# The first scale and shift as TensorE products in four column tiles, and two projection units multiplied tile by tile

## Chip, cores and metric

One NeuronCore of a Trainium2 chip runs the whole program. The metric is device time in microseconds (us) of one execution.

## The reference

A trunk of two layers, 256 tokens of 1024 channels, all in float32. What the change touches is the beginning of layer 0:

```python
cond = jax.nn.silu(c)
for l in range(DEPTH):
    sh1, sc1, g1, sh2, sc2, g2 = jnp.split(cond @ ada_w[l] + ada_b[l], 6, axis=-1)
    hn = rmsnorm(x, norm_mix_w[l]) * (1.0 + sc1[:, None]) + sh1[:, None]
...
        mix = mixer_ab(hn, ab_w_in[e], ...)
    x = x + g1[:, None] * mix
```

`mixer_ab` projects `hn` with `ab_w_in`, runs attention with sinks on one part and a gated DeltaNet on another (a short causal convolution with SiLU on q, k and v, then the delta rule in chunks of 64), and projects back. A dense SwiGLU, a second mixer, a top-2-of-8 expert SwiGLU and a final norm follow.

## The kernel before

All weights stream from HBM in units of 1 MB (128 partitions of 2048 floats) through five `raw` buffers. One queue, SyncE's (SP), issues every load in program order, and a load waits until the unit that was in its buffer has been read. The engines each run their instructions in order; a scheduler sets that order from the program and its own estimates, except inside `manual_schedule`, where the program's order stands.

A float32 product is made of three products of 32-bit halves. `split` makes the halves of a weight: ACT casts `raw` to `hi` (128x1024 at a time), DVE subtracts to get `lo` (two pieces of 128x512). `mm3` then issues hi by hi, lo by hi and hi by lo. The norm's output is kept as eight channel tiles (128 channels by 256 tokens), each again as `xhi` and `xlo`. So a unit of 256 output channels costs two halves of 8 tiles by 3 products, 48 matmuls.

At the start, `ada_first` makes the first scale (`Ac`) and shift (`shc`), two channel tiles at a time. The weight unit lies in HBM transposed (`adaw`), and DVE multiplies it by the SiLU row `crow` and sums along the row, one instruction per channel tile with `junk` as its output. `norm_T` is interleaved with this by its `before` callback: it scales x by the root mean square into `xs0` and `xs1`, PE turns each channel tile (two transposes into a PSUM tile `cb`), ACT writes `xhi` from it with scale and shift, ACT (for tiles 0 to 3) or DVE (4 to 7) writes the float32 `fk`, and DVE subtracts for `xlo`.

`mixer_ab` then multiplies unit by unit: first the small unit `abs` (beta and decay inputs, 24 products, since it fills one half), then the two k units (`abw[1]`, `abw[2]`), whose `sink` copies the result to `cpad`, applies the four convolution taps (one on ACT, three on DVE, `cv`), SiLU and the squares for the l2 norm. From the small unit come beta and g by a softplus of some twenty small DVE instructions, and from g the decay matrices `DT`; k and `DT` go into the `pair` products, and a long chain of small steps that inverts a triangular matrix follows. The q, v and attention units are fillers, pumped into that chain.

## Time and profile before

| | |
|---|---|
| median of 3 runs | 1418.18 us (1418.10 to 1418.77) |
| the profiled execution | 1417.63 us |
| its span in the trace | 1415.80 us |
| PE, DVE, ACT busy | 1349.7, 971.5, 727.6 us |
| mean rate from HBM | 340 GB/s |

The span runs from the first to the last instruction of the trace; 1.83 us of the execution lie around it. Times in the trace count from the start of the span. A matmul's time in a row holds its way through the array, so that the spacing of two matmuls' starts, not their length, is what one costs in a stream.

### The profile page before, as it was taken

What the parts mean: (1) busy time and instruction counts of PE and PEld (TensorE: products, weight loads), DVE (VectorE), ACT (ScalarE), POOL (GpSimd) and SP (SyncE); (2) the same over time, 40 slices, a digit from 0 to 9 for tenths busy, and PEclk for the clock granted to TensorE, in tenths of its full rate; (3) what the DMA queues carried; (4) which work ended last, traced back from release to release, by engine and by line L of the source; (5) the groups of instructions that cost most, each with busy time, mean ns of one, the idle gap of its engine ahead of it and who ended that gap; (6) DMA issues with size and microseconds to landing.
All of it is one profiled execution on the core that took longest, in us unless ns stands there. A gap on an engine that the chain in (4) does not pass through costs nothing.

```text
span 1415.8 us, 22845 instructions
## 1 busy us (share of the span) xinstructions
PE 1349.7 (95%) x8894; PEld 1031.7 (73%) x8894; DVE 971.5 (69%) x1373; ACT 727.6 (51%) x1003; POOL 13.0 (1%) x25
## 2 busy tenths in 40 slices
PE   2989998999989999999999999999999999999996
PEld 1888677999979986687666766667766677666762
DVE  7899878878987965787556665557655567465542
ACT  5865527444457754676444554445544555344531
POOL 0010000000000000000000000000000000000000
PEclk9999999999999999999999999999999999999998
DMA  9548356879773423999999999999999999999994
GB/s 374 200 153 323 124 187 265 319 284 409 298 273 135 148 91 119 383 426 426 425 426 424 425 426 425 426 425 427 424 426 426 425 426 425 427 425 426 424 426 191
DMA packets 68662, 482.71 MB, mean 341 GB/s; under 512 B 7873, under 2 KB 8257, under 8 KB 10689
## 3 DMA queue, kind: packets, MB, share of 16 engines
q1 hardware_dynamic: 66816, 477.19, 82.4%
q10 hardware_dynamic: 1728, 3.97, 0.8%
q8 instruction: 72, 1.18, 0.3%
q14 instruction: 46, 0.37, 0.1%
HBM read 479.03 MB, written 2.10 MB: 340 GB/s over the span
## 4 chain that ended last, share of the span: by engine, by line
PE 86%; DVE 8%; ACT 3%; issue 1%; DMA 1%; SPq 0%; ACTq 0%; DVEq 0%
PE gu L1426 14%; PE gu L219 10%; PE gu L221 10%; PE gu L220 10%; PE dnh L1448 7%; PE dn L219 5%; PE dn L221 5%; PE dn L220 5%; PE pj L221 3%; PE pj L219 2%; PE pj L220 2%; PE ms L1476 2%; DVE lo L205 1%; DVE ajunk L248 1%; PE cb L221 1%
## 5 line engine op out<-in xcount | busy, mean ns | idle before, releaser
L205 DVE TENSOR_TENSOR lo<-raw,hi 128x1024 fp32r<-128x1024 f32 (+1 forms) x496 | 578.5, 1178 | 188.1 <-ACT hi L200 178.8
L200 ACT CAST hi<-raw 128x1024 fp32r<-128x1024 f32 x473 | 490.7, 1049 | 339.6 <-DMA raw<-in_md 101.6
L1426 PE MATMUL gu<-raw,xq 128*64 128x256 f32 x1792 | 207.5, 382 | 0.0
L219 PE MATMUL gu<-hi,xeh 128*128 128x512 f32 x448 | 181.0, 404 | 0.0
L1426 PEld LDWEIGHTS gu<-raw,xq 128*64 128x64 f32 x1792 | 125.1, 137 | 75.1 <-issue 18.5
L220 PE MATMUL gu<-lo,xeh 128*128 128x512 f32 x448 | 177.6, 396 | 0.0
L221 PE MATMUL gu<-hi,xel 128*128 128x512 f32 x448 | 177.4, 396 | 0.0
L221 PE MATMUL pj<-xhi,lo 128*128 128x256 f32 x376 | 107.2, 287 | 6.5 <-DVE lo L205 6.3
L219 PE MATMUL pj<-xhi,hi 128*128 128x256 f32 x376 | 107.2, 286 | 5.4 <-ACT hi L200 5.4
L220 PE MATMUL pj<-xlo,hi 128*128 128x256 f32 x376 | 106.8, 285 | 0.0
L1448 PE MATMUL dnh<-raw,hq 128*64 128x512 f32 x448 | 103.6, 600 | 0.5 <-ACT hq L1480 0.5
L219 PEld LDWEIGHTS gu<-hi,xeh 128*128 128x128 f32 x448 | 84.4, 188 | 21.2 <-issue 3.0
L219 PE MATMUL gu<-xhi,hi 128*128 128x256 f32 x352 | 99.5, 283 | 0.0
L221 PE MATMUL gu<-xhi,lo 128*128 128x256 f32 x352 | 99.0, 281 | 0.4 <-DVE lo L205 0.4
L221 PEld LDWEIGHTS gu<-hi,xel 128*128 128x128 f32 x448 | 84.5, 189 | 20.3
L232 DVE SCALAR_TENSOR_TENSOR ajunk<-raw,crow 128x1024 bf16<-128x1024 f32 x80 | 98.5, 1231 | 0.9
L220 PE MATMUL gu<-xlo,hi 128*128 128x256 f32 x352 | 98.9, 281 | 0.0
L220 PEld LDWEIGHTS gu<-lo,xeh 128*128 128x128 f32 x448 | 84.6, 189 | 18.2
L1469 DVE TENSOR_TENSOR h<-sg,gu 128x256 f32<-128x256 f32 (+1 forms) x56 | 30.8, 550 | 87.2 <-PE gu L221 78.8
L219 PE MATMUL dn<-hi,hh 128*128 128x512 f32 x224 | 90.1, 402 | 0.0
L220 PE MATMUL dn<-lo,hh 128*128 128x512 f32 x224 | 87.5, 391 | 0.0
L221 PE MATMUL dn<-hi,hl 128*128 128x512 f32 x224 | 87.5, 391 | 0.0
(450 smaller groups left out, 1872.8 us busy)
## 6 DMA issues: line engine op xcount, KB each, us to landing
raw<-in_mg SPq DMA_DIRECT2D x112, 1024.0 KB, 19.5
raw<-in_mu SPq DMA_DIRECT2D x112, 1024.0 KB, 19.5
raw<-in_md SPq DMA_DIRECT2D x110, 1024.0 KB, 19.5
raw<-in_adaw SPq DMA_DIRECT2D x48, 1024.0 KB, 8.9
raw<-in_fgu SPq DMA_DIRECT2D x22, 1024.0 KB, 7.5
raw<-in_cdw SPq DMA_DIRECT2D x14, 1024.0 KB, 5.5
raw<-in_fdn SPq DMA_DIRECT2D x11, 1024.0 KB, 7.1
raw<-in_abw SPq DMA_DIRECT2D x9, 1024.0 KB, 7.8
```

The source lines that it names most:

```text
L200: self.nc.scalar.copy(hv, src)
L205: self.nc.vector.tensor_tensor(lv[z], src[z], hv[z].bitcast(F32), op=ALU.subtract)
L219: mm(ps, lh, rh, start=first, stop=False)
L220: mm(ps, lh, rl, start=False, stop=False)
L221: mm(ps, ll, rh, start=False, stop=last)
L232: nc.vector.scalar_tensor_tensor(junk, raw[:, h], 1.0, self.crow, op0=ALU.mult, op1=ALU.mult, accum_out=dst[:, q:q + 1])
L248: nc.vector.scalar_tensor_tensor(junk, raw[:, h], 1.0, self.crow, op0=ALU.mult, op1=ALU.mult, accum_out=dst[:, 2 * u + h:2 * u + h + 1])
L1426: nc.tensor.matmul(gu[name, i][q * HALF:q * HALF + HALF, 0:256], xf[:, kk], w[:, k, q * 256:q * 256 + 256], start=kk == 0, stop=kk == 7)
L1448: nc.tensor.matmul(acc[e][h * HALF:h * HALF + HALF], st[i][:, k % 2, k // 2 * HALF:k // 2 * HALF + HALF], w[:, 0, h * 512:h * 512 + 512], ...
L1469: nc.vector.tensor_tensor(h, st[i], gu.pop(('mu', i))[:, 0:m], op=ALU.mult)
L1476: nc.tensor.transpose(ps[:, q], h[:, q * P:(q + 1) * P], ident)
```

## The change

The scale and shift weights of the first norm now lie in HBM as they do for a projection (`adaf`, channels by 256 outputs). `ada_first` multiplies them on PE: for each of the eight channel blocks one float32 matmul whose stationary operand is the block's SiLU column, broadcast to 32 columns, so that block k goes to column tile k mod 4 and to a quarter of the PSUM partitions. ACT copies the 256 sums out (`asum`), and a matmul of one column with `sums` (ones on partitions 0, 32, 64 and 96) adds the four quarters and turns them into a column. DVE adds the bias.

`first` replaces the interleaved `norm_T`. Under `manual_schedule` it goes through four rounds: scale and shift of two channel tiles, their transposes, `xhi` and `xlo`, then those tiles' products with the two k units, which are loaded ahead of the small unit. Their sums stay open in four PSUM tiles (three `pj` and the one `ms`) over all rounds. `mixer_ab` gets the finished sums as `begun`, and the small unit comes after them. All eight `fk` and both halves of `xs1` are DVE's now.

```diff
+    A['adaf'] = blocks(f['ada_w'][0][:, :2 * D], 256)
...
-    def ada_first(self, A, sh):
+    def ada_first(self, wk, u, A, sh, sums):
...
-        for u in range(4):
-            z = slice(2 * u, 2 * u + 2)
-            for j, dst in ((1, A), (0, sh)):
-                raw = self.raw(self.A['adaw'][j * 4 + u])
-                for h in range(2):
-                    junk = self.ap.tile([P, D], BF16, name="ajunk", bufs=1)
-                    nc.vector.scalar_tensor_tensor(junk, raw[:, h], 1.0, self.crow, op0=ALU.mult, op1=ALU.mult,
-                                                   accum_out=dst[:, 2 * u + h:2 * u + h + 1])
...
+        for i, (j, dst) in enumerate(((1, A), (0, sh))):
+            raw = self.first_raw.pop(0)
+            h = slice(i * 256, i * 256 + 256)
+            for k in range(8):
+                q = slice(k % 4 * 32, k % 4 * 32 + 32)
+                nc.tensor.matmul(ps[q, h], self.cc[:, k:k + 1].to_broadcast([P, 32]), raw[:, k], start=k < 4, stop=k >= 4)
+            nc.scalar.copy(sb[:, h], ps[:, h])
+            for c in range(2 * i, 2 * i + 2):
+                nc.tensor.matmul(pc[:, c:c + 1], sb[:, c * P:(c + 1) * P], sums, start=True, stop=True)
+            nc.vector.tensor_tensor(dst[:, z], pc[:, 2 * i:2 * i + 2], self.col('ada', j * 8 + 2 * u, 2), op=ALU.add)
...
+    def first(self, wk, A, sh):
...
+        todo = [W['adaf'][4], W['adaf'][0], W['abw'][1], W['adaf'][5], W['adaf'][1], W['abw'][2],
+                W['adaf'][6], W['adaf'][2], W['adaf'][7], W['adaf'][3]]
...
+        def tile_(k):
+            p = turned.pop(k)
+            fk = wk.tile([P, T], F32, name="fk", tag="Ub", bufs=2)
+            nc.scalar.activation(hi[:, k], p, AF.Identity, bias=sh[:, k:k + 1], scale=A[:, k:k + 1])
+            nc.vector.tensor_scalar(fk, p, A[:, k:k + 1], sh[:, k:k + 1], op0=ALU.mult, op1=ALU.add)
+            nc.vector.tensor_tensor(lo[:, k], fk, hi[:, k].bitcast(F32), op=ALU.subtract)
+
+        def halves(u):
+            for s in range(2):
+                w.append(self.split(units[u][:, :, s * P:s * P + P]))
+
+        def times(k, us):
+            for u in us:
+                for i in (2 * u, 2 * u + 1):
+                    hv, lv = w[i]
+                    self.mm3(ps[i], (hv[:, k], lv[:, k]), (hi[:, k], lo[:, k]), k == 0, k == 7)
+
+        with self.tc.manual_schedule():
+            self.ada_first(wk, 0, A, sh, sums)
+            fetch(2)
+            turn(0), turn(1)
+            tile_(0), tile_(1)
+            halves(0)
+            fetch(1)
+            times(0, (0,)), times(1, (0,))
+            self.ada_first(wk, 1, A, sh, sums)
+            fetch(2)
+            turn(2), turn(3)
+            tile_(2), tile_(3)
+            times(2, (0,)), times(3, (0,))
+            halves(1)
+            for k in range(4):
+                times(k, (1,))
+            self.ada_first(wk, 2, A, sh, sums)
+            turn(4), turn(5)
+            tile_(4), tile_(5)
+            times(4, (0, 1)), times(5, (0, 1))
+            turn(6), turn(7)
+            self.ada_first(wk, 3, A, sh, sums)
+            tile_(6), tile_(7)
+            times(6, (0,)), times(7, (0,)), times(6, (1,)), times(7, (1,))
...
-        kn, gk = conv_in(0, 1, "kn", rk)
+        kn, sink = conv_in(0, 1, "kn", rk)
+        for u in range(2):
+            sink(u, begun[u])
         small()
-        for _ in gk:
-            pass
...
-                xT = self.norm_T(wk, Ac, shc, busy=True, before=before)
-                self.mixer_ab(xT, wk, g1, Ac2, shc2)
+                xT, begun = self.first(wk, Ac, shc)
+                self.mixer_ab(xT, begun, wk, g1, Ac2, shc2)
```

The order of the instructions shows three places. Numbers behind a name are buffers. First PE, in the kernel before: after the last transposes of the norm come the products of the small unit (`hi_262`, `lo_263`), one channel tile after the other.

```order
L309 MATMUL cb_240<-konst_71,xs1_146 128x128
L309 MATMUL cb_247<-konst_71,xs0_145 128x128
L309 MATMUL cb_247<-konst_71,xs1_146 128x128
L219 MATMUL pj_267<-xhi_151,hi_262 128x256
L220 MATMUL pj_267<-xlo_152,hi_262 128x256
L221 MATMUL pj_267<-xhi_151,lo_263 128x256
```

PE in the changed kernel, second round: the scale's eight products (`raw_123`), the two with `sums`, the shift's (`raw_125`), four transposes, and then the products of tiles 2 and 3 with the first k unit (`hi_202`, `hi_207`).

```order
L249 MATMUL cb_226<-raw_123,cc_81 32x256 x8
L252 MATMUL cb_228<-sums_127,asum_227 128x1 x2
L249 MATMUL cb_226<-raw_125,cc_81 32x256 x8
L252 MATMUL cb_228<-sums_127,asum_227 128x1 x2
L292 MATMUL cb_261<-konst_71,xs0_142 128x128
L292 MATMUL cb_261<-konst_71,xs1_143 128x128
L292 MATMUL cb_264<-konst_71,xs0_142 128x128
L292 MATMUL cb_264<-konst_71,xs1_143 128x128
L217 MATMUL pj_150<-xhi_148,hi_202 128x256
L218 MATMUL pj_150<-xlo_149,hi_202 128x256
L219 MATMUL pj_150<-xhi_148,lo_203 128x256
```

What was one block of transposes and one block of products is cut into rounds; each `L252` reads the `asum` that ACT copies from the `cb` of the row ahead of it.

Second, DVE where the norm ends. Before, the small unit's halves (`lo_263`) lie between the last weight sums, and the first k unit's (`lo_305`, `lo_334`) directly behind the last two norm tiles, with the small unit's result (`ab`).

```order
L248 SCALAR_TENSOR_TENSOR ajunk_223,shc_89<-raw_219,crow_75 128x1024
L205 TENSOR_TENSOR lo_263<-raw_260,hi_262 128x512
L250 TENSOR_TENSOR shc_89<-shc_89,colp_72 128x2
L205 TENSOR_TENSOR lo_263<-raw_260,hi_262 128x512
L315 TENSOR_SCALAR fk_243<-cb_240,Ac_88,shc_89 128x256
L315 TENSOR_SCALAR fk_250<-cb_247,Ac_88,shc_89 128x256
L316 TENSOR_TENSOR xlo_152<-fk_243,xhi_151 128x256
L316 TENSOR_TENSOR xlo_152<-fk_250,xhi_151 128x256
L205 TENSOR_TENSOR lo_305<-raw_299,hi_304 128x512
L425 COPY ab_255<-cb_294 128x32
```

In the changed kernel the same place has the last two norm tiles, the small unit's halves (`lo_504`), both k units' convolutions, and only then the halves of the next unit (`lo_699`, `lo_728`) and the small unit's result.

```order
L253 TENSOR_TENSOR shc_89<-cb_395,colp_72 128x2
L298 TENSOR_SCALAR fk_421<-cb_387,Ac_88,shc_89 128x256
L299 TENSOR_TENSOR xlo_149<-fk_421,xhi_148 128x256
L298 TENSOR_SCALAR fk_425<-cb_390,Ac_88,shc_89 128x256
L299 TENSOR_TENSOR xlo_149<-fk_425,xhi_148 128x256
L203 TENSOR_TENSOR lo_504<-raw_501,hi_503 128x512 x2
L471 SCALAR_TENSOR_TENSOR cv_459<-cpad_460,colp_72,cv_459 128x256 x6
L471 SCALAR_TENSOR_TENSOR cv_459<-cpad_480,colp_72,cv_459 128x256 x6
L203 TENSOR_TENSOR lo_699<-raw_696,hi_698 128x512 x2
L203 TENSOR_TENSOR lo_728<-raw_696,hi_727 128x512 x2
L506 COPY ab_455<-cb_535 128x32
```

The convolutions moved ahead of the small unit's result and of the next unit's halves. Third, ACT in the changed kernel's last two rounds and behind them.

```order
L250 COPY asum_322<-cb_321 128x256 x2
L297 ACTIVATE xhi_148<-cb_349,shc_89,Ac_88 128x256
L297 ACTIVATE xhi_148<-cb_352,shc_89,Ac_88 128x256
L640 ACT_TABLE_LOAD
L640 ACTIVATE ea_569<-rowp_74 128x8
L250 COPY asum_394<-cb_393 128x256 x2
L297 ACTIVATE xhi_148<-cb_387,shc_89,Ac_88 128x256
L297 ACTIVATE xhi_148<-cb_390,shc_89,Ac_88 128x256
L198 CAST hi_503<-raw_501 128x1024
L465 COPY cpad_460<-pj_150 128x256
L469 ACTIVATE cv_459<-pj_150,colp_72 128x256
```

The cast of the small unit (`raw_501`) stands behind the last tile of the norm, and the copies of the k units' results behind it.

## Rows read from the trace of the kernel before

**Rows 1.** The page: busy tenths in 40 equal slices, 35.4 us each.
```profile
PE   2989998999989999999999999999999999999996
```

**Rows 2.** Chain of waits in order of time: start us, us, what.
```profile
1.67 6.29 DMA x<-in_x
...
10.73 1.15 DVE ajunk L248 x2
...
33.06 1.22 DVE ajunk L248 x2
...
34.94 0.58 PE pj L221
...
38.09 0.21 PE pj L219
...
38.82 0.12 PE pj L220
...
564.03 9.46 DMA raw<-in_mg
...
652.52 3.60 PE gu L1426 x32
```

**Rows 3.** Stretch, length, busy us (instructions) of PE, PEld, DVE, ACT, POOL; granted clock, DMA.
```profile
55.00:60.00 5.00, 5.00 (x49) 4.91 (x48) 4.52 (x12) 4.30 (x6) 2.12 (x3) 1.00 0.25 100
60.00:65.00 5.00, 5.00 (x45) 5.00 (x44) 3.58 (x10) 4.96 (x9) 0.87 (x1) 1.00 0.51 162
65.00:70.00 5.00, 5.00 (x19) 2.61 (x18) 3.86 (x8) 4.94 (x6) 0.10 (x1) 1.00 0.11 48
70.00:100.00 30.00, 26.07 (x299) 23.38 (x299) 30.00 (x65) 18.72 (x29) 3.80 (x4) 1.00 0.38 128
...
sum 95.00, PE 90.76 PEld 83.60 DVE 87.75 ACT 65.11 POOL 10.18; mean PE 10.08 PEld 9.29 DVE 9.75 ACT 7.24 POOL 1.13
```

**Rows 4.** Timeline: start us, us, engine line op out<-in xcount [idle before <-releaser].
```profile
11.85 0.29 ACT L286 ACTIVATE rstd<-rstd,eps 128x2 f32<-128x2 f32 x1
13.25 0.72 ACT L297 ACTIVATE xs<-x,rstd 128x512 f32<-128x512 f32 x1 [1.11 <-DVE rstd L287]
16.23 0.56 ACT L311 ACTIVATE xhi<-cb,shc,Ac 128x256 fp32r<-128x256 f32 x1 [0.42 <-PE cb L309]
17.29 0.43 DVE L316 TENSOR_TENSOR xlo<-fk,xhi 128x256 fp32r<-128x256 f32 x1
29.05 0.54 DVE L315 TENSOR_SCALAR fk<-cb,Ac,shc 128x256 f32<-128x256 f32 x1
29.11 1.04 ACT L200 CAST hi<-raw 128x1024 fp32r<-128x1024 f32 x1
34.88 0.68 DVE L205 TENSOR_TENSOR lo<-raw,hi 128x512 fp32r<-128x512 f32 x1
39.44 0.36 ACT L421 COPY abT<-pj 16x256 f32<-16x256 f32 x1 [2.43 <-PE pj L221]
39.85 0.29 PE L424 MATMUL cb<-konst,abT 16*128 16x16 f32 x2 [0.22 <-ACT abT L421]
51.59 0.57 ACT L381 COPY cpad<-pj 128x512 f32<-128x512 f32 x1
54.10 2.46 DVE L390 SCALAR_TENSOR_TENSOR cv<-cpad,colp,cv 128x256 f32<-128x256 f32 x6
432.21 1.10 PE L987 MATMUL cb<-xc,lga 128*128 128x256 f32 x4
```

**Rows 5.** Busy time by stretch while the first weights land (columns as in rows 3).
```profile
10.00:15.00 5.00, 0.97 (x4) 0.65 (x5) 4.32 (x11) 3.87 (x7) 0.00 (x0) 1.00 1.01 424
```

**Rows 6.** Busy time by stretch around a change of the granted clock (PEclk).
```profile
154.80:158.20 3.40, 1.54 (x12) 1.24 (x12) 2.72 (x8) 3.34 (x10) 0.00 (x0) 0.97 0.40 169
158.20:161.60 3.40, 3.40 (x16) 1.82 (x16) 2.14 (x6) 2.23 (x6) 0.00 (x0) 0.53 0.02 5
161.60:165.00 3.40, 3.40 (x46) 2.39 (x45) 1.89 (x4) 0.66 (x2) 0.00 (x0) 1.00 0.36 84
```

More of the change, by code (lines that the diff above doesn't have):

```diff
@@ new lines, in first, with fetch, turn @@
+    def first(self, wk, A, sh):
+        nc, W = self.nc, self.A
+        nc.sync.dma_start(self.x, W['x'])
+        todo = [W['adaf'][4], W['adaf'][0], W['abw'][1], W['adaf'][5], W['adaf'][1], W['abw'][2],
+                W['adaf'][6], W['adaf'][2], W['adaf'][7], W['adaf'][3]]
+        self.first_raw, units = [], []
+        def fetch(n):
+            for _ in range(n):
+                src = todo.pop(0)
+                (units if len(todo) in (7, 4) else self.first_raw).append(self.raw(src))
+            if not todo:
+                self.late()
+        fetch(5)
+        sums = wk.tile([P, 1], F32, name="sums")
+        nc.vector.tensor_reduce(sums, self.kc('ident')[:, 0:P:32], axis=AX.X, op=ALU.add)
+        r = self.rstd(wk)
+        xs = [wk.tile([P, D], F32, name=f"xs{t}", tag=tg) for t, tg in enumerate(("kbe", "kdec"))]
+        for h in range(2):
+            hs = slice(h * 512, h * 512 + 512)
+            nc.scalar.activation(xs[0][:, hs], self.x[:, 0, hs], AF.Copy, scale=r[:, 0:1])
+            nc.vector.tensor_scalar(xs[1][:, hs], self.x[:, 1, hs], r[:, 1:2], None, op0=ALU.mult)
+        hi = self.xtp.tile([P, 8, T], F32R, name="xhi", tag="xhi")
+        lo = self.xtp.tile([P, 8, T], F32R, name="xlo", tag="xlo")
+        ps = [self.psp.tile([P, 512], F32, name="pj", bufs=3)[:, 0:T] for _ in range(3)]
+        ps.append(self.psm.tile([P, 512], F32, name="ms")[:, 0:T])
+        w = []
+        turned = {}
+        def turn(k):
+            turned[k] = self.psp.tile([P, T], F32, name="cb", bufs=4)
+            for t in range(2):
+                nc.tensor.transpose(turned[k][:, t * P:(t + 1) * P], xs[t][:, k * P:(k + 1) * P], self.kc('ident'))
+        def tile_(k):
[36 more added lines that the diff above has]
+            times(6, (0,)), times(7, (0,)), times(6, (1,)), times(7, (1,))
+        return (hi, lo), (ps[:2], ps[2:])
@@ L288, in rstd, with norm_T @@
         return r
-    def norm_T(self, pool, Acol, shcol, tags=("kbe", "kdec"), busy=False, before=None):
+    def norm_T(self, pool, Acol, shcol, tags=("kbe", "kdec")):
         nc = self.nc
@@ L380, in sink @@
                 nc.gpsimd.memset(pad[:, :, 0:3], 0.0)
-                nc.scalar.copy(pad[:, :, 3:], ps)
+                if b:
+                    nc.scalar.copy(pad[:, :, 3:], ps)
                 us = slice(2 * u, 2 * u + 2)
@@ L384, in sink @@
                     q = 2 * u + s
+                    p = ps[:, s] if b else ps[s]
+                    if not b:
+                        nc.scalar.copy(pad[:, s, 3:], p)
                     def w(tap):
                         return self.col('dnc', tap * 12 + w0 * 4 + q)
-                    nc.scalar.activation(cv[:, q], ps[:, s], AF.Copy, scale=w(3))
+                    nc.scalar.activation(cv[:, q], p, AF.Copy, scale=w(3))
                     for tap in range(3):
@@ L406, in sink @@
                         nc.vector.reciprocal(nrm, nrm)
-            return cv, self.proj_chan([A['abw'][1 + 2 * b + v] for v in range(2)], xT, sink)
+            return cv, sink if b == 0 else self.proj_chan([A['abw'][1 + 2 * b + v] for v in range(2)], xT, sink)
         va = wk.tile([P, 2, P], F32, name="va")
```

31 lines of the change are left out of this document (9 added, 22 removed).

## Prediction

> **What bounds the kernel now.** I read the page's slices first [rows 1]: PE is at 9 or more tenths nearly everywhere, and the first slice of 35 us holds the one long stretch in which it has almost nothing to do. The whole change lies there. The chain of waits over that stretch [rows 2] says what is waited for: x lands at 7.96, its squares run on ACT, and from 10.73 to 34.28 it is DVE alone, with sixteen products of adaLN weights by the silu row (`ajunk`, two to a scale or shift of two channel tiles). PE's steady stream of projection products begins at 34.94. From there, two things are to be seen. Products of 256 columns follow each other every 0.21 us at first, which is 1.2 GHz, and every 0.12 us from about 38.5, which is 2.4 GHz [rows 2]; the column of the granted clock reads 1.00 in all of that stretch, and I go by the spacing. And the engines are all full: the windows from 35 to 130 us [rows 3] show DVE at 30.00 of 30.00 us from 70 to 100 and at 87.75 of the 95 in all. So after 35 the stage is paid in DVE time, with PE close behind, and a gain at the start counts only as far as DVE and PE reach the same state sooner. Such a shift reaches the end in full: the first expert weights are waited for at 564 [rows 2], after a routing that needs everything ahead of it.
>
> The state to compare is the one in which all eight norm tiles, the small unit (`abs`, 24 products) and the two k units (96 products) are done. Before, ACT starts to copy the second k unit out at 51.59 [rows 4], so these 120 products end at about 51.5.
>
> **What is removed.** DVE's sixteen products of 1.22 us, some 20 us, and with them the queue in which a norm tile's low part waited behind them. DVE gets xs1 (two halves, about 0.45 us each) and all eight `fk` instead of four. Both lie where DVE now waits.
>
> **What is added on PE.** For each weight unit (eight of them) there are eight f32 matmuls of 256 columns in four column tiles, one ACT copy, two matmuls of one column, and small DVE adds. No row shows four tiles. The nearest are one tile, four matmuls of this shape in 1.10 us, about 0.235 us apart [rows 4], and two tiles, 32 in 3.60 us, 0.1125 us each at 2.4 GHz [rows 2]. Doubling the tiles halved the price, so I take 0.056 us at 2.4 GHz and 0.11 us at 1.2 GHz; the other end is that four tiles run no better than two. Eight then take 0.45 or 0.86 us. Behind them come some 0.25 us until the result is out and seen, 0.37 us for the copy (0.36 for `abT`, and 0.05 from its end to PE's next start), and 0.3 us for the two short ones (0.29 for the pair of L424) [rows 4]. One half is 1.35 us at 2.4 GHz and 1.85 us at 1.2 GHz. The rows of the order show why nothing fills it: PE runs in order, and L252 stands directly behind its own eight, waiting for ACT.
>
> The Trainium skill, "TensorE: Matmul & The Clock Gate", section "Measured speedup vs the span model", measures 2.38 times for three column tiles, not 3. By it four tiles would make about 3.2 times, an estimate, and the 64 matmuls would cost 1 to 2 us more; the sum below would be about +5 instead of +3.7. No row here shows four tiles.
>
> **The start, step by step.** The weights are not late. A unit is 1.05 MB, the queue moves 424 GB/s [rows 5], so units land about 2.5 us apart after x's 7.96: 10.4, 12.9, and so on to about 32.8 for the last scale-or-shift unit. The first of them waits for ACT: the root is done at 12.14, then come the reciprocal and two xs halves (0.72 us each, about 0.62 apart) [rows 4], and in ACT's order the first copy stands behind these, at 13.6. From there, by rows 4 (xhi 0.56, fk 0.54, xlo 0.43, cast 1.04, lo 0.68 us):
> Round 1: second half done at 16.2; four transposes; first low tile at 18.4; the first unit's casts stand behind two xhi on ACT (17.8 to 19.8), its low parts on DVE come at 19.8 and 21.0; twelve products until 22.5.
> Round 2: two halves at 1.85 us to 26.2; transposes; low tile at 28.4; twelve products to 30.8; then 24 products of the other unit. These 36 are the first stretch in which PE is full, so I let the clock rise at about 32; they end at 34.2.
> Round 3: two halves at 1.35 us to 36.9; low tile 38.8; 24 products, partly at 1.2 GHz, to 43.1.
> Round 4: transposes, two halves to 46.2; low tiles to 48.9; 24 products to 51.0.
> Then the small unit's 24 (2.8 us) to 53.8. So the 120 products end about 2.3 us later than now, although the first began 15 us earlier: half of the time between 13.6 and 51 PE waits for a copy, an add or a tile.
>
> The clock is the weak term. The windows around 158 [rows 6] show what PE did before it fell and rose here: with 1.54 of 3.40 us busy it fell from 2.4 to 1.2 GHz, and after a stretch that was full it was back. Rounds 3 and 4 are of the first sort in part. With 1.2 GHz for all four rounds, the same steps end at 58.3; with 2.4 GHz for all of them at 45.8.
>
> **The sum.** DVE's ledger, since DVE is the full engine. Work between 35 and 130 before: 87.75 us [rows 3]. Of it, done in the changed kernel by the last low tile: eight lo halves of the k units (5.0 us) and two fk and two xlo (1.7 us). Of the small unit's two lo, about 0.75 us ran before 35 and is now still to do. Left: 81.8 us. From 48.9 that reaches 130.7, against 130: +0.7 us if DVE never waits again. It will: between 55 and 70 it is idle for 15.00 - 4.52 - 3.58 - 3.86 = 3.04 us, in the chain from the small unit through g and the decay matrices [rows 3]. That chain starts at 39.4 now (`abT`) [rows 4], and at 53.8 after the change, behind the k units rather than ahead of them, with less other work to lay beside it. I let 3.0 us recur: **+3.7 us**. All 7.25 us of idle between 35 and 130 would make +8.0. A second account agrees in sign: in DVE's new order twelve convolution steps (2.46 us for six [rows 4]) stand ahead of the next unit's lo, so PE, done with the small unit at 53.8, waits until about 57 for work that it has at 51.6 now; against that, six of those steps are done sooner.
>
> The profiled execution took 1417.63 us and the median of the runs is 0.55 us above it. 1417.63 + 3.7 is 1421.3, so the median should be **1421.9 us**, 0.26% slower. Below about 0.2% (2.8 us) a measurement of this kernel can't be told from no change.
>
> **The rivals.**
> *Clock at 1.2 GHz throughout, or tiles that don't overlap.* The first makes the rounds end at 58.3, the second (0.1125 us a matmul) at 53 to 58: +6 to +11 us, up to 1429. For it: the clock fell at 158 after a stretch with waits in it, and the rounds are made of such stretches [rows 6]. Against it: the 36 products of round 2 are as full as the stretch at 35 after which the clock rose. Chance 0.15. The Trainium skill, the same page, section "HAM oscillation — how this bites in real kernels", speaks against the change: bursts of matmuls between waits each begin at the low clock. The rise and fall around 158 agree.
> *Clock at 2.4 GHz from the second round on, DVE's waits as before.* Rounds end at 45.8 to 47, the last low tile at 43.7 to 45: the ledger gives -1.5 to 0 us, about 1417.5, no change that can be measured. Chance 0.20.
> *The same clock, and DVE's waits vanish*, since the k units' convolutions and the next splits now fill the gaps of the chain from the small unit. 43.7 + 81.8 is 125.5: -4.5 us, 1413.7, faster by 0.3%. It decides as soon as the last low tile comes before about 45 and DVE is never idle for more than a microsecond until 130. For it: 33 more projection products stand ahead of the first pair products of the delta rule in the new order. Against it: those three idle microseconds are waits for ACT and POOL, which no DVE order fills. Chance 0.15.
> That the change does nothing can be left out: the order shows every instruction moved.
>
> **How the numbers follow.** My forecast (rounds ending between 49 and 53, +1 to +7 us, 1419 to 1425) has 0.45, the three rivals 0.15, 0.20 and 0.15; 0.05 is for none of these. Slower by over 0.2%: most of the forecast (0.38), the first rival, a little of the rest, 0.54. Within 0.2%: the second rival and the low end of the forecast, 0.29. Faster: the third rival and the rest, 0.17. The range from 1415 to 1427 leaves out the far ends of the first and third rivals. The likeliest case alone is 1419 to 1425.
>
> **What would show it.** In the profile after: no `ajunk` before 90 us; the first asum copy at 13.6; eight column-tile matmuls in 0.9 us at first; PE's waits in the rounds for ACT's asum and DVE's xlo; the last xlo at 48 to 50 and the cast of `abs` about there; products of 0.21 us until some 32; DVE's work of 130 at 131 to 135. The prediction is wrong if the rounds end before 46, if two copies of asum stand closer than 2.5 us in rounds 2 to 4, or if DVE is full from 49 to 70.

## The result and the profile after

The changed kernel took **1438.5 us** (median of four runs, 1437.7 to 1439.4) against 1418.1 us: a ratio of 1.0145, 95% interval 1.0132 to 1.0158, or 20.35 us slower. The forecast was 1421.9 us with a range to 1427. The direction was right and the size far too small. The profiled execution took 1438.4 us, with a span of 1436.6 us. Three single executions of 2700 to 6544 us, where all others took 1411 to 1445, are left out of every median below.

The page after, which answers to [rows 1], has these slices of 35.9 us each, and below them stands the granted clock of before:

```profile
PE   6889998999998999999999999999999999999996
PEclk9899999999999999899999999999999999999998
```

```profile
PEclk9999999999999999999999999999999999999998
```

PE's first slice went from 2 tenths to 6, as it should, and the second from 9 to 8. The clock now dips in the second slice, which it didn't before.

The timeline of the rounds and of what comes behind them (columns as in [rows 4]):

```profile
17.80 1.09 PE L292 MATMUL cb<-konst,xs 128*128 128x128 f32 x4
...
24.68 1.87 PE L249 MATMUL cb<-raw,cc 128*32 128x256 f32 x16
26.68 0.37 ACT L250 COPY asum<-cb 128x256 f32<-128x256 f32 x1 [5.27 <-PE cb L249]
...
27.64 1.07 PE L249 MATMUL cb<-raw,cc 128*32 128x256 f32 x16
...
29.67 1.03 PE L292 MATMUL cb<-konst,xs 128*128 128x128 f32 x4
...
38.34 1.07 PE L249 MATMUL cb<-raw,cc 128*32 128x256 f32 x16
39.95 0.61 PE L252 MATMUL cb<-sums,asum 128*128 128x1 f32 x4 [0.55 <-ACT asum L250]
40.49 1.07 PE L249 MATMUL cb<-raw,cc 128*32 128x256 f32 x16
...
42.52 0.64 PE L292 MATMUL cb<-konst,xs 128*128 128x128 f32 x4
...
47.45 0.60 PE L292 MATMUL cb<-konst,xs 128*128 128x128 f32 x4
...
51.70 0.61 PE L252 MATMUL cb<-sums,asum 128*128 128x1 f32 x4 [0.49 <-ACT asum L250]
...
54.63 0.42 DVE L299 TENSOR_TENSOR xlo<-fk,xhi 128x256 fp32r<-128x256 f32 x1
...
58.17 0.28 PE L219 MATMUL ms<-xhi,lo 128*128 128x256 f32 x1
...
58.38 4.84 DVE L471 SCALAR_TENSOR_TENSOR cv<-cpad,colp,cv 128x256 f32<-128x256 f32 x12
63.13 2.49 DVE L203 TENSOR_TENSOR lo<-raw,hi 128x512 fp32r<-128x512 f32 x4
63.87 0.58 PE L219 MATMUL pj<-xhi,lo 128*128 128x256 f32 x1 [2.39 <-DVE lo L203]
65.00 0.35 ACT L502 COPY abT<-pj 16x256 f32<-16x256 f32 x1
65.53 1.70 PE L483 MATMUL cb<-konst,sq 128*128 128x2 f32 x8
70.36 0.39 PE L505 MATMUL cb<-konst,abT 16*128 16x16 f32 x2
70.78 0.19 DVE L506 COPY ab<-cb 128x32 f32<-128x32 f32 x1 [5.16 <-PE cb L505]
```

Three things are to be seen. The eight matmuls of a half (L249) are **sixteen** rows of the trace, and the two sums behind them (L252) four: an f32 matmul is two rows. A half takes 2.15 us from one L249 group to the next, at 2.4 GHz. The last low tile is done at 55.05, not 48.9. And behind it, PE pauses for 2.39 us up to 63.87: the low halves of the first q unit stand on DVE behind all twelve convolution steps of the k units.

The windows behind the rounds (columns as in [rows 3]):

```profile
55.00:150.35 95.35, 88.23 (x903) 80.48 (x902) 82.00 (x182) 60.83 (x102) 9.36 (x11) 0.92 0.50 182
55.00:60.00 5.00, 5.00 (x36) 5.00 (x36) 2.89 (x8) 3.91 (x10) 0.00 (x0) 0.79 0.31 102
60.00:65.00 5.00, 2.61 (x18) 2.41 (x17) 5.00 (x13) 4.97 (x8) 0.21 (x2) 0.89 0.50 193
65.00:70.00 5.00, 5.00 (x25) 5.00 (x25) 0.62 (x2) 2.75 (x5) 0.00 (x0) 0.50 0.65 208
70.00:75.00 5.00, 5.00 (x27) 4.74 (x27) 3.07 (x13) 3.10 (x5) 0.00 (x0) 0.59 0.02 5
75.00:80.00 5.00, 4.68 (x40) 4.48 (x38) 2.48 (x11) 3.55 (x6) 0.00 (x0) 1.00 0.00 0
```

The first row is the stretch of 35 to 130 of before, moved by the 20.35 us at its end and cut at the last low tile. DVE has 82.00 us of work in it. From 65 to 75 PE is full, at a granted clock of 0.50 and 0.59, and DVE is busy for 3.69 of 10 us.

For the experiments I read two more points. The first is the start of the first `kbe` on DVE, near the end of the triangular solve of the delta rule, whose last step on DVE starts 1.3 to 6.9 us later, by the kernel. It comes at 157.0 before and 176.4 after, +19.4 us, so nearly all of the loss lies ahead of it; the rest of the span is 1258.8 and 1260.2 us. The second is PE's first product of the solve's result with `kbe`, which needs both. It comes at 168.1 before and 186.2 after, +18.1 us:

```profile
L766 PE MATMUL cb<-TT,kbe x64: 217/219/268, 168.1 to 172.1; 64*64 64x64 f32 x64
L847 PE MATMUL cb<-TT,kbe x64: 218/218/267, 186.2 to 190.1; 64*64 64x64 f32 x64
```

From the end of the last low tile to the first `kbe`, before and after:

```profile
37.30:157.00 119.70, 113.09 (x1311) 101.32 (x1310) 107.89 (x233) 84.56 (x151) 10.18 (x11) 1.00 0.59 212
```

```profile
55.05:176.44 121.39, 112.06 (x1247) 99.82 (x1246) 103.39 (x228) 81.32 (x150) 9.36 (x11) 0.94 0.52 186
```

This is the row that the prediction lacked. PE, not only DVE, is nearly full here: 113.09 of 119.70 us. After the change it has 64 instructions fewer to make (not 96: 19 of the k units' products and all 24 of the small unit's still lie behind its last low tile), yet is busy for about as long, since 112.06 us at a mean clock of 0.94 are only some 105.3 at full clock, and it is idle for 9.33 us and not 6.61. So +19.4 is 17.75 (last low tile later) - 7.8 (less work for PE) + 6.7 (low clock) + 2.7 (idle). The clock has two digits, so the parts are good to about half a microsecond.

### The profile page after: what moved, and what is told of

Same layout as the page of the kernel before. It is cut to its first block, busy times and chain, and to the rows that moved or that the text cites. A ratio compares the mean times of both kernels' runs of the same rounds, so it can differ in the third digit from the quotient of the medians.

```text
span 1436.6 us, 23148 instructions
## 1 busy us (share of the span) xinstructions
PE 1376.8 (96%) x9054; PEld 1049.5 (73%) x9054; DVE 956.4 (67%) x1348; ACT 725.9 (51%) x1006; POOL 12.2 (1%) x25
## 4 chain that ended last, share of the span: by engine, by line
PE 87%; DVE 7%; ACT 4%; issue 2%; DMA 0%; SPq 0%; ACTq 0%; DVEq 0%
PE gu L1507 14%; PE gu L217 10%; PE gu L219 10%; PE gu L218 10%; PE dnh L1529 7%; PE dn L217 5%; PE dn L219 5%; PE dn L218 5%; PE pj L219 2%; PE pj L218 2%; PE pj L217 2%; DVE lo L203 2%; PE ms L1557 2%; PE cb L218 1%; PE cb L217 1%
```

## The experiments

The theories are told in the expectations: A, the small unit comes too late; B, the rounds; C, PE's pauses and its clock; D, what DVE's queue puts ahead of g; E, DVE's own work. All runs in one table: the ratio to the kernel before with its 95% interval, and, in us from the profiled execution, the end of the last low tile, the start of the first `kbe` and the start of its first product. From `kbe` to the end the kernels take 1255.7 to 1263.9 us, and from its first product 1246.0 to 1251.4, which I did not explore; so the right columns tell more than the ratio.

These marks come from one execution each, and they scatter. Five kernels have rounds that are written the same (changed, small unit first, series first, filled pause, q unit early), and their last low tile is done at 54.8 to 57.2. What differs is the clock: in the changed kernel the products of round 2 follow each other every 0.21 us until 36.4, in series first until 38.7, and in q unit early they come every 0.12 us from 32 on and slow down at about 44. So a last low tile that moves by less than 2.4 us shows nothing by itself.

| kernel | median us | ratio | last low tile | first kbe | first kbe product |
|---|---|---|---|---|---|
| before | 1418.1 | | 37.3 | 157.0 | 168.1 |
| changed | 1438.5 | 1.0145 (1.0132 to 1.0158) | 55.1 | 176.4 | 186.2 |
| no halves | 1415.6 | 0.9978 (0.9962 to 0.9993) | 36.0 | 153.4 | 164.6 |
| halves alone | 1428.8 | 1.0086 (1.0065 to 1.0108) | 41.5 | 166.6 | 177.7 |
| products alone | 1425.7 | 1.0060 (1.0040 to 1.0080) | 48.1 | 168.3 | 178.0 |
| small unit first | 1440.0 | 1.0166 (1.0143 to 1.0189) | 54.8 | 178.5 | 189.7 |
| series first | 1439.0 | 1.0154 (1.0124 to 1.0184) | 57.2 | 177.5 | 188.7 |
| grouped halves | 1434.8 | 1.0131 (1.0107 to 1.0155) | 54.5 | 174.9 | 184.6 |
| filled rounds | 1436.8 | 1.0117 (1.0090 to 1.0143) | 54.4 | 175.1 | 188.8 |
| half of the sum | 1433.9 | 1.0100 (1.0082 to 1.0118) | 53.6 | 174.2 | 184.2 |
| filled pause | 1437.5 | 1.0126 (1.0110 to 1.0143) | 55.2 | 173.9 | 187.6 |
| both filled | 1433.6 | 1.0101 (1.0084 to 1.0118) | 57.1 | 175.2 | 185.7 |
| q unit early | 1434.1 | 1.0114 (1.0097 to 1.0131) | 55.1 | 169.9 | 180.6 |
| grouped, q early | 1435.3 | 1.0119 (1.0103 to 1.0136) | 57.0 | 171.8 | 182.6 |
| split work | 1421.8 | 1.0024 (1.0014 to 1.0033) | 35.9 | 160.2 | 170.0 |
| split, k early | 1418.9 | 1.0005 (0.9996 to 1.0014) | 35.3 | 155.9 | 166.7 |

### The two parts of the change apart

**Halves alone.** Scale and shift on PE in the rounds, no product there; the small unit and the k units come behind, as before.

```diff
-            halves(0)
-            times(0, (0,)), times(1, (0,))
...
+        kn, gk = conv_in(0, 1, "kn", rk)
...
+        for _ in gk:
+            pass
...
```

> The halves on PE as in the changed kernel, but no projection product in the rounds: the small unit first and then the two k units, as in the kernel before. Theory A: the norm tiles are done at 40 to 45 (before: 37.3), ab follows at 46 to 49 (before: 40.2), and the time is 4 to 9 us above before, 1422 to 1427. Theory B: halves on PE cost what the changed kernel costs, whatever stands between them: 10 us or more above before, 1428 to 1438.

Measured: 10 us slower than before, at the border of theory B's range. The last low tile comes only 4.2 us later; the other 5.4 us up to `kbe` are lost behind it.

**Products alone.** DVE makes scale and shift as before; the k units' products stay in the rounds.

```diff
-                nc.tensor.matmul(ps[q, h], self.cc[:, k:k + 1].to_broadcast([P, 32]), raw[:, k], start=k < 4, stop=k >= 4)
+                nc.vector.scalar_tensor_tensor(junk, raw[:, h], 1.0, self.crow, op0=ALU.mult, op1=ALU.mult,
+                                               accum_out=dst[:, 2 * u + h:2 * u + h + 1])
...
```

> The other half of the change alone: scale and shift stay with DVE, as in the kernel before, and only the two k units' products are interleaved with the norm tiles; the small unit comes behind them. No halves stand on PE. DVE has the 20 us of products by the silu row and now also the k units' eight low halves, 5.0 us, ahead of the last low tile, which I expect at 42 to 45 (before: 37.3). Theory A, the order alone costs: with the 13 us of DVE's idle time of the changed kernel the time is 1423 to 1430. Theory C, the clock: products come 12 to 36 at a time between DVE's stretches, at 1.2 GHz, and the pause behind the small unit is as in the changed kernel: the same 1423 to 1430, with a granted clock below 0.7 in the 10 us behind the small unit. Theory B, only the halves on PE cost: 1417 to 1421.

Measured: `kbe` 11.3 us later than before, the last low tile 10.8 us later (48.1, where 42 to 45 was expected). The time is in the range that theories A and C share, and above theory B's. The sign that theory C named besides is there: from 58 to 68 us, behind the small unit, PE is full at a granted clock of 0.51. So each part loses by itself, without the other.

**No halves.** The scale and shift columns come from a loaded column and the bias, with no product at all.

```diff
-                nc.tensor.matmul(ps[q, h], self.cc[:, k:k + 1].to_broadcast([P, 32]), raw[:, k], start=k < 4, stop=k >= 4)
...
+            nc.vector.tensor_tensor(dst[:, z], raw[:, 0, 0:2], self.col('ada', j * 8 + 2 * u, 2), op=ALU.add)
```

> Leaves out the scale and shift products with the silu row: the scale and shift columns are made from a loaded weight column and the bias alone, so PE and ACT are spared the eight column-tile halves, and all else is in the changed kernel's order. The rounds should then end near 40 to 46. Theory B: the halves are the loss, and the time falls below that of before, to 1408 to 1416. Theory A: the k units still stand ahead of the small unit, with ab some 12 us behind the rounds, so ab comes at 52 to 58, 12 to 18 us later than before, and the time stays above before: 1420 to 1428.

Measured: in theory B's range, but hardly below before: with nothing to pay for scale and shift, the last low tile is done at 36.0, sooner than expected, and `kbe` comes 3.6 us before that of before. From tile to `kbe`:

```profile
36.00:153.39 117.39, 107.14 (x1245) 94.60 (x1243) 103.58 (x227) 81.56 (x151) 9.37 (x11) 0.99 0.61 221
```

PE has some 7 us less to do than before, and 3.6 us more of idle time. In this order of the rest, the k units' products ahead of time are worth 2.3 us between these two points.

### Is it the place of the small unit? (theories A and D)

**Small unit first.** Its products go to another PSUM buffer, and it is written ahead of the k sinks.

```diff
+        small()
         for u in range(2):
             sink(u, begun[u])
-        small()
```

> Theory A (the small unit's place): the changed kernel loses most because the small unit's result comes behind the k units' convolutions, their tables on ACT and their norm sums on PE: ab at 70.78 although its products end near 61.3. Here the small unit is emitted ahead of the two k sinks. ab should come at 62 to 64, g, the decay matrices and U 6 to 9 us sooner, and the time fall by 6 to 9 us, to 1430 to 1433. Theory B (the rounds): the loss is that the rounds end at 58.5 and everything behind is fixed to that; the rounds are untouched, so at most 2 us come back, 1436 to 1439.

**Series first.** The same, and `beta`, the softplus series and `g` written ahead of the k sinks too.

> In all kernels so far some 120 us lie between the last low tile and the first kbe, whether the k units are done by then or not. Theory D (the queue): DVE's queue threads the softplus series (sgq) through the convolutions and low halves of the unit that comes next; in the changed kernel that is the first q unit, whose 48 products PE has yet to make, so g waits for PE, and the work done ahead in the rounds buys nothing. Here the small unit and the whole series up to g are written ahead of the two k sinks, so that DVE's order has the series in one piece: g should come at 69 to 73 in place of 83.77, U 7 to 12 us sooner, kbe at 165 to 170 and the time fall to 1427 to 1432. Theory C (the clock and PE's load behind the rounds): PE is full at 1.2 GHz from 64 to 74 either way; g comes sooner, but kbe by at most 3 us: 1434 to 1438.

Measured in the first: `ab` at 62.05 in place of 70.78, as theory A has it, and `kbe` 2 us *later*, with a time of 1440.0 us, above both ranges. In the second, the rows of the tiles `g`, `U` and `kbe` (last numbers: first and last start):

```profile
L529 DVE SCALAR_TENSOR_TENSOR g<-sgq,ea x1: 174/174/174, 72.2 to 72.2; 128x16 f32<-128x16 f32 x1
L713 DVE TENSOR_TENSOR U<-cb,DB x2: 685/686/687, 85.1 to 85.7; 128x512 f32<-128x512 f32 x2
L817 DVE TENSOR_TENSOR kbe<-cb,beg x2: 680/686/691, 177.5 to 178.7; 128x512 f32<-128x512 f32 x2
```

`g` comes 11.6 us sooner and `U` 12.9 us sooner than in the changed kernel, just as theory D says, and `kbe` 1.1 us later. Its last low tile came 2.1 us later too, so from there to `kbe` it took 1.1 us less (120.3 us for 121.4). The time is 1439.0 us. Theories A and D fall: the chain through g can be pulled forward by 12 us, and hardly anything follows. PE's windows show where it went:

```profile
85.00:90.00 5.00, 2.02 (x15) 1.61 (x14) 5.00 (x7) 2.03 (x3) 3.38 (x3) 1.00 0.00 0
90.00:95.00 5.00, 2.98 (x3) 1.00 (x4) 5.00 (x10) 1.72 (x2) 0.10 (x1) 0.51 0.00 0
```

Now PE waits for DVE's `E` (4.4 us in two waits), and its clock falls there.

### Is it the rounds? (theory B)

**Grouped halves.** Both products of a round first, then both pairs of sums: the loop over scale and shift is split in two ahead of the sums.

> Scale's and shift's eight matmuls of a round are issued together, and the one-column sums behind both copies, so PE waits once in a round for ACT and not twice. Rounds end some 0.8 us sooner each, 55 to 56 in place of 58.5. Theories A and B both let the end follow the rounds one to one: 1435 to 1436.5. A third theory C, that the granted clock in the rounds is what costs, expects a larger gain or none, by whether the denser matmuls move the rise and the fall of the clock; under it the rounds' end moves by more than 4 us or by less than 1.

Measured: last low tile 0.6 us sooner, not 2.5 to 3.5; `kbe` 1.5 us sooner. By the expectation's words that is theory C's sign (less than 1 us), but a move within the scatter decides nothing.

**Filled rounds.** Extra matmuls where PE waits for ACT's copy.

```diff
+            for k in range(4):
+                q = slice(k * 32, k * 32 + 32)
+                nc.tensor.matmul(pc[q, 256:512], self.cc[:, k:k + 1].to_broadcast([P, 32]), raw[:, k], start=True, stop=True)
```

> Repeats four of the eight column-tile matmuls of each half into unused columns, ahead of the one-column sums, where PE waits some 0.5 us for ACT's copy: 32 more matmuls, 0.5 us a half at 2.4 GHz, half of it or all of it in the wait. Theory C: the stretches at 1.2 GHz from 30 to 36.4 and from 53.5 to 57 go, the last low tile comes 2 to 5 us sooner and the time is 1433 to 1437. Theory B (the halves' own time): PE is the engine that the rounds wait for, and the added matmuls make them end 1 to 4 us later: 1439 to 1443.

**Half of the sum.** Four matmuls in a half, for eight.

```diff
-            for k in range(8):
+            for k in range(4):
...
-                nc.tensor.matmul(ps[q, h], self.cc[:, k:k + 1].to_broadcast([P, 32]), raw[:, k], start=k < 4, stop=k >= 4)
+                nc.tensor.matmul(ps[q, h], self.cc[:, k:k + 1].to_broadcast([P, 32]), raw[:, k], start=True, stop=True)
```

> Leaves out the second half of each sum of scale and shift: four column-tile matmuls in each half, not eight, which as each shows as two rows is eight rows of 0.055 us, the number that the forecast had for the whole half. If the mis-counted rows are what delayed the rounds (theory B), the last low tile comes 4 to 6 us sooner, at 49 to 51 as forecast, and the first kbe as much sooner, at 171 to 173 (176.44). If the rounds wait for something else (ACT's copy, DVE's adds, the clock), the last low tile moves by less than 2 us.

Both measured in the stretch from 13 us to the last low tile, the filled rounds first, then half of the sum, then the changed kernel itself:

```profile
13.00:54.40 41.40, 34.35 (x295) 23.59 (x295) 14.13 (x36) 12.26 (x23) 0.00 (x0) 1.00 0.80 300
```

```profile
13.00:53.60 40.60, 31.47 (x178) 23.70 (x178) 14.13 (x36) 12.12 (x22) 0.00 (x0) 0.87 0.81 310
```

```profile
13.00:55.05 42.05, 32.40 (x237) 23.53 (x238) 14.13 (x36) 12.46 (x23) 0.00 (x0) 0.90 0.81 300
```

The clock column can't be trusted here: it reads 1.00 up to 25 us in every kernel, and in series first up to 55, where the products follow each other every 0.21 us (1.2 GHz) until 38.7. So I go by the spacing. From 13 us to the last low tile, the filled rounds have some 15 us at 1.2 GHz, the changed kernel 23 and half of the sum 28. With more matmuls the clock stays up from 28 us on; with fewer it is low for longer, and PE is busy for nearly as long. The halved kernel's L249 groups do take 0.64 us and not 1.07, but its products of the first form average 427 ns where the changed kernel's average 382. The rounds end within 1.5 us of each other, less than the scatter. So theory B's 4 to 6 us for the mis-counted rows didn't come, and theory C's 2 to 5 us for the clock didn't either (the filled rounds' time, 1436.8 us, is in theory C's range, but its runs lie between 1431.7 and 1440.7). As far as one execution of each can show it, the one gives back what the other takes.

### Is it PE's pause and its clock behind the rounds? (theories C and E)

**Filled pause.** The small unit's 24 products once more, into unused columns.

```diff
+            for k in range(8):
+                self.mm3(ps[:, T:2 * T], (hv[:, k], lv[:, k]), (xT[0][:, k], xT[1][:, k]), k == 0, k == 7)
```

> Repeats the small unit's 24 products into unused columns, 2.8 us of extra work at 2.4 GHz, placed where PE waits from 61.3 to 63.87 in the changed kernel. Theory C (the clock behind the rounds): that wait is what lets the clock fall to 1.2 GHz from 64 to 74, where PE is full and DVE idles; with the wait filled, the stretch from 64 on runs at 2.4 GHz, DVE's idle time behind the last low tile falls by 4 to 7 of its 13.35 us, and the time falls to 1431 to 1435 although PE has more to do. Theory A (the order of the small unit and the k units): the clock is a side issue, DVE's idle time stays and the time is 1437 to 1441.

Measured: PE has 24 products more, and `kbe` comes 2.5 us sooner. The windows, and then a stretch behind `kbe`, here and in the changed kernel (columns as in [rows 4]):

```profile
60.00:65.00 5.00, 5.00 (x45) 5.00 (x44) 5.00 (x12) 4.97 (x7) 0.21 (x2) 1.00 0.49 190
65.00:70.00 5.00, 5.00 (x37) 4.84 (x36) 2.69 (x8) 4.92 (x8) 0.00 (x0) 0.81 0.60 208
```

```profile
182.16 2.67 PE L608 MATMUL pj<-pT,va 128*64 128x128 f32 x14
181.70 1.74 PE L606 MATMUL pj<-pT,va 128*64 128x128 f32 x14
```

The pause is gone and the clock stays up until after 65. Both kernels that fill the pause reach `kbe` 118.7 and 118.1 us after the last low tile, where the six other kernels with halves and products in the rounds and without the q unit early take 120.3 to 123.7. But what was won at `kbe` is lost again behind it: the clock falls there (0.65 from 175 to 188, and 1.00 from 174 to 187 in the changed kernel), the same 14 rows take 2.67 us and not 1.74, and the first product of `kbe` comes at 187.6, 1.4 us later than in the changed kernel. The time, 1437.5 us, is in theory A's range and not in theory C's, and DVE's idle time from the last low tile to `kbe` falls by 2.3 us (18.0 to 15.7), not by 4 to 7. So this run doesn't show that filling the pause pays in the end. **Both filled** was to show whether the gains add:

> Both fillings together. Theory C: the two gains add, 1427 to 1432. Theories A and B: both fillings only cost, 1438 to 1445.

It was 1433.6 us, just above theory C's range, but its last low tile was done at 57.1, 2.7 us later than in the filled rounds by themselves, and its `kbe` came at 175.2; the time is better than the stage, and I draw nothing from it.

**q unit early.** No work more or less: the q unit's casts and low halves are written ahead of the k sinks.

```diff
+        abs_ = self.split(self.raw(A['abs']))
+        ahead = list(self.halves(A['abw'][3], 'c'))
         for u in range(2):
             sink(u, begun[u])
-        small()
+        small(abs_)
+        self.ahead = [ahead]
...
```

> All work of the changed kernel, no more and no less; the casts and low halves of the first q unit stand ahead of the k units' copies and convolutions on ACT and DVE, so PE goes on from the small unit's products to the q unit's without the pause from 61.3 to 63.87. Theory C (PE is the bound behind the rounds, and a pause on PE costs its own time and then the low clock): of PE's 9.3 us of idle time and 7.6 us lost at the low clock between the last low tile and the first kbe, 5 to 9 us go, kbe comes at 168 to 172 and the time is 1430 to 1434. Theory E (DVE is the bound): DVE's work is the same and only in another order, so kbe moves by less than 2 us: 1436 to 1440.

```profile
55.00:60.00 5.00, 3.80 (x22) 3.60 (x20) 2.94 (x6) 3.62 (x6) 0.00 (x0) 0.72 0.32 100
60.00:65.00 5.00, 4.88 (x41) 4.88 (x42) 5.00 (x13) 4.74 (x10) 0.11 (x1) 1.00 0.94 385
65.00:70.00 5.00, 4.93 (x42) 4.69 (x41) 3.56 (x10) 4.97 (x8) 0.11 (x1) 1.00 0.06 25
70.00:75.00 5.00, 5.00 (x45) 5.00 (x45) 2.80 (x11) 4.93 (x10) 0.00 (x0) 1.00 0.55 190
```

```profile
L850 PE MATMUL cb<-TT,kbe x64: 217/219/268, 180.6 to 184.8; 64*64 64x64 f32 x64
```

From 65 to 75 PE makes 87 instructions, where the changed kernel made 52, both with PE full. It waits ahead of 60 instead, so that from 55 to 75 it makes 150 for 106; at 0.12 us each, the spacing at 2.4 GHz, these 44 are some 5 us, an estimate. `kbe` comes at 169.9, 6.6 us sooner. Two steps of the solve now stand behind it, so the first product of `kbe` is the better mark here, 5.6 us sooner. The time falls by 4.4 us to 1434.1, with an interval that just doesn't touch the changed kernel's; those of half of the sum and of both filled don't either, while their marks hardly moved, so it is the marks that carry this. Theory E, which gave less than 2 us, falls. Theory C's forecast holds here, although the edit takes away the wait and the slow stretch together and can't price them apart.

### Towards a version that is faster

**Grouped, q early:** the two edits together.

> The two edits that helped, together: scale's and shift's matmuls of a round grouped, and the first q unit's low halves ahead of the convolutions. Theory C (PE's ledger): the first kbe is the last low tile, plus PE's work at 2.4 GHz, plus its idle time, plus what the low clock costs it. With the last low tile at 54.5 and some 115 us behind it, as with the q unit early alone, kbe comes at 168 to 171 and the time is 1429 to 1434. Theory E (DVE is the bound): the gains don't add and kbe stays at 172 or later.

Nothing was added: the last low tile was done at 57.0 here, and behind it all was as with the q unit alone (114.8 us from the last low tile to `kbe` in both, and 125.6 and 125.5 to its first product). The eight kernels with halves and products in the rounds and without the q unit early take 118.1 to 123.7 us to `kbe` and 128.6 to 134.9 to its first product. So the gain of the q unit early came twice; that of the grouped halves didn't.

**Split work.** Scale on DVE as before and shift on PE, both at work in one round; no products in the rounds, and the small unit and the k units behind them as before. **Split, k early** also lets DVE make the next round's scale ahead of this round's low tiles, and casts the first k unit ahead of the small unit's result. Lines of the second:

```diff
+            for u in range(4):
+                turn(2 * u), turn(2 * u + 1)
+                if u < 3:
+                    next(ada[u + 1])
+                tile_(2 * u), tile_(2 * u + 1)
...
+        abs_ = self.split(self.raw(A['abs']))
+        self.ahead = [list(self.halves(A['abw'][1], 'c'))]
...
```

> A kernel of another cut: scale stays with DVE, 8 products of 1.22 us, and shift goes to PE in four column tiles, so that both work on a round at once; no projection product in the rounds, the small unit and the k units behind them as in the kernel before. The eight weight units land some 2.5 us apart, the last at about 28, and PE's half is 3.4 us at 1.2 GHz, so the last low tile should come at 32 to 34 (before: 37.3). If the 120 us from there to kbe are constant, kbe comes at 152 to 154 and the time is 3 to 5 us below before, 1413 to 1416. If any half on PE costs as much as in the kernel with the halves alone (+10 us with all eight), the last tile comes at 36 to 38 and the time is 1418 to 1423.

> Scale on DVE and shift on PE, as in the kernel with the split work, with two edits by PE's ledger: DVE makes the next round's scale ahead of this round's low tiles, so the last low tile should come at 31 to 34 (before: 37.3), and the first k unit's casts and low halves stand ahead of the small unit's result, so PE has no pause behind the small unit. Theory C: 31 to 34, plus 113 us of work, 6.6 to 8 us idle and 0 to 3 at the low clock make kbe 151 to 157 (before: 157.0) and a time of 1412 to 1418. Theory E: DVE, which has 108 us of work behind the last low tile here as before, with its 11.8 us of idle time, gives 151 to 154 at best, and only if its waits stay; the two differ where PE's clock falls: then theory C has kbe at 157 or later and theory E not.

Measured: the first is 0.24% slower than before, the second no different. The first's last low tile came at 35.9, not 32 to 34, and its `kbe` at 160.2, not 152 to 154; the time, 1421.8 us, is in the expectation's other case, in which a half on PE costs as much as in the halves alone. The second's last tile comes 2.0 us sooner than that of before and `kbe` 1.1 us, and neither reaches the end. Its `kbe`, at 155.9, is in theory C's range and 1.9 us behind the best case that theory E named, and the time is 1 us above theory C's range, so I don't count it for either. No kernel that does all the work is measurably faster than the one before.

## Why the prediction was right in sign and wrong in size

**What bounds the kernel, and the ledger.** DVE's work was forecast at 81.8 us behind the last low tile and measured at 82.00. The sum was 48.9 + 81.8 + 3.0 against 130; measured it is 55.05 + 82.00 + 13.35 against the same 130, or +20.4. The window's end was set by the measured loss, so this divides the loss and doesn't prove it. By it two terms failed, by 6.15 and 10.35 us.

**First failed term: "Eight then take 0.45 or 0.86 us".** The price of a row was about right and the count was wrong. I read L987 in [rows 4], four rows in 1.10 us, as four matmuls of one tile; its loop issues two. With four column tiles the sixteen rows take 1.07 us, and (1.07 - 0.38) / 15 is 0.046 us between rows, where I had 0.056 (0.38 us is the shortest single row). So the four tiles do overlap. They do so better than the Trainium skill's three would give scaled up ("TensorE: Matmul & The Clock Gate", section "Measured speedup vs the span model"), an estimate: 0.235 / 3.2 is 0.073 a row, and 1.48 us by the same sum. The two sums of one column are four rows, 0.61 us and not 0.3; the wait for the copy was about right (0.55 us for 0.62). A half at 2.4 GHz is 2.15 us for the 1.35 of the text. In the rows of the rounds, the halves of round 1 end at 17.80 and not at 16.2; those of rounds 2 and 3 take 4.99 and 4.18 us (24.68 to 29.67, 38.34 to 42.52) and not 3.7 and 2.7; those of round 4 with their transposes 4.86 us (47.45 to 52.31) and not 3.1. That is 6.1 us in all, which is the size by which the rounds came late; what lay between came out even. The rounds' halves as a whole are a large cost: without them (no halves) the last low tile is done 19.05 us sooner. What the runs don't confirm is that the mis-counted rows by themselves set the end of the rounds: with half of them the last low tile came only 1.5 us sooner, while the clock was low for longer. A kernel with fewer rows *and* a clock that stays up wasn't run.

**Second failed term: "I let 3.0 us recur".** I counted the waits of DVE and took PE's place beside it as given, though [rows 3] show PE at 90.76 of 95 us. DVE's 3.04 us of idle time before were no property of the chain from the small unit; the chain can move by 12 us almost without effect (series first). And they were not waits for ACT and POOL, as the text has it against its third rival: more than half of them were for PE. In the trace of before, between 55 and 70 us (total, times, longest):

```profile
DVE E L603 <- PE cb L595: 1.1, 1, 1.1
DVE cv L390 <- ACT cv L388: 0.7, 1, 0.7
DVE egl L612 <- ACT egl L578: 0.6, 1, 0.6
DVE gc L574 <- PE cb L570: 0.5, 1, 0.5
```

Before, PE is busy for all of the time from 40 to 75 us, at 2.4 GHz from 38.5 [rows 2]; after, it pauses for 2.39 us at 61.5, and then makes the q unit at 1.2 GHz until about 74, with DVE waiting. I had weighed the clock in the rounds only. The text did name the pause ("twelve convolution steps stand ahead of the next unit's lo, so PE ... waits until about 57"), and priced it at its own length. With the slow stretch behind it, it cost more: when only the order was changed, 5.6 us came back at the first product of `kbe`. Of the 10.35 us, 4.4 come back in the time that way; the rest is spread over shorter waits and low-clock stretches (one around 105: granted clock 0.67 from 105 to 110), and no run here assigns it.

Such a pause isn't always followed by a slow stretch. Before, PE waits longer, 3.01 us for DVE's `E`, and the products behind it go on at 0.12 us:

```profile
80.76 1.10 PE L647 MATMUL cb<-E,konst 128*128 128x512 f32 x2 [3.01 <-DVE E L644]
81.81 0.28 PE L220 MATMUL pj<-xlo,hi 128*128 128x256 f32 x1
81.93 0.28 PE L221 MATMUL pj<-xhi,lo 128*128 128x256 f32 x1
```

Why the clock fell behind the one and not behind the other, no run here shows.

**The clock in the rounds.** Forecast: 1.2 GHz until 32, then high. By the rows, the third L249 group at 24.68 still takes 1.87 us and the fourth at 27.64 1.07; then the clock is low again from 30 to 36.4 and from 53.5 to 57. Up to the last low tile that is some 23 us of it from 13 on, and not 19: the moments were wrong, the amount nearly right. But rounds written the same had it at other moments (series first until 38.7), so no fixed moment could have been right.

**The rivals.** The one with the low clock throughout (up to 1429 us) was the nearest, and still 9.5 us short. Its rounds end at 58.3, and they did end at 58.5, but by luck: they had 2.4 GHz for some 21 of the 48 us from 10 on. That the ledger gives +11 us at most for such an end, and not +20, is the second failed term again. The section of the Trainium skill that stood beside it ("TensorE: Matmul & The Clock Gate", "HAM oscillation — how this bites in real kernels": work that comes in bursts starts each at the low clock) agrees with the trace at a place where I hadn't applied it, behind the rounds (1.2 GHz from 63.87 on, after the pause of 2.39 us). With the trace before, behind the pause of 3.01 us, it doesn't agree. The two rivals with the clock at 2.4 GHz from the second round on fall: the filled rounds, with 32 matmuls more, have it from 28 us on, and their last low tile is at 54.4, not at 43.7 to 45.

**The signs that were named.** Held: the first `asum` copy at 13.16 (13.6), the waits of PE for ACT's copy, 5.2 us in the rounds. Missed: the last low tile (55.05 for 48 to 50), DVE's work at 150 (131 to 135). One test was badly put: copies of asum closer than 2.5 us were to refute the sum, yet the sum itself had them 1.35 to 1.85 us apart. They are 2.10 us apart, and the halves are too long, not too short.

## What to carry to other kernels

Write the ledger for every engine that is nearly full, not only for the fullest, and look behind each of TensorE's pauses for a slow stretch: here 2.4 us of waiting and the stretch at 1.2 GHz behind it cost some 5.6 us, while a pause of 3.0 us before had no such stretch. Where a mark in the trace has moved, read a second one behind it, and see how far the mark scatters in kernels that are the same up to it. Count the instructions in the program, and take their prices from the trace: a row of the trace is not always one matmul. And before work is moved ahead of a barrier, ask what the freed engine would do with the time: with the products of scale and shift left out altogether, making 96 products early moved the end of the stage by only 3.6 us.

## What was not expected of the hardware

An f32 matmul of 128x256 shows as two rows, with one column tile as with four (L987: two matmuls, four rows; L249: eight, sixteen). Four column tiles of 32 took 1.07 us for eight such matmuls, against 1.10 us for two with one tile. And rounds that are written the same didn't get the same clock: in five kernels the last low tile came at 54.8 to 57.2, the latest where the products stayed at 0.21 us until 38.7. Matmuls that do no useful work are not shown to pay: with 32 of them in the rounds, one kernel had some 15 us at 1.2 GHz in place of 23 and its last low tile 0.65 us sooner, but another with the same rounds (both filled) had some 22 and a last low tile at 57.1; 24 behind the rounds brought `kbe` 2.5 us forward, but not its first product.
